# Two half-GLU chunks by seven products, and a reordered last branch, in a hybrid encoder layer on one core

## The chip, the core and the metric

The kernel runs on one core of a Trainium2 chip. The metric is device time in microseconds (us): what one execution of the whole program takes, from its start on the device to its end. Four engines matter here besides the DMA queues: PE (TensorE, matrix products), DVE (VectorE) and ACT (ScalarE), which evacuate accumulators and prepare operands, and POOL (GpSimd), which does a few elementwise operations and issues DMAs. SP only issues DMAs, here those that load weights. Each engine works through its own instructions strictly in the order in which they stand in its queue, and waits at an instruction until all that it needs is there.

## The reference

One encoder layer for 768 tokens (two request groups, of 256 and 512), model width 1024, all in float32. Of its parts only these bear on the change:

```python
y = (y_f + y_b).reshape(Bsz, L, S5_WIDTH) + s5_d * uf      # state space model
z = jax.nn.gelu(y)
s5_out = z * jax.nn.sigmoid(z @ s5_w_glu)                  # the half-GLU
# three branches (0: s5_out, 1: differential attention, 2: memory attention)
# each: merged += sigmoid(gate_n) * (branch_n @ w_branch[n])
# then x + merged @ w_out, RMSNorm, SwiGLU FFN, residual
```

`s5_w_glu` and each `w_branch[n]` are 1024 x 1024.

## The kernel before, in words

**Products.** Activations lie feature by token: a "row" is 128 features by 768 tokens, so an operand of width 1024 has eight rows, k = 0 to 7. A float32 operand is kept as a high and a low half in a rounded format, made by ACT (a copy that rounds: "hi") and DVE (the operand less that: "lo"); a product is three matmuls (`mm3`, L755 hi by hi, L756 hi by lo, L757 lo by hi), summed in PSUM.

**Weights.** `WStream` brings weights in chunks of 256 output columns. SP loads two raw tiles per chunk (128 x 1024, tag "wr", three buffers, L539). A plain chunk is split by ACT (L599) and DVE (L605), two instructions of 128 x 1024 each. A chunk of kind "w2" is split by `_split_w` for seven products: four sums and differences of weight blocks by POOL (L574, L575, L581, L583), and seven factors A11, A12, S2, S1, S3, S4, A22 by ACT (L557) and DVE (L558), 128 x 512 each, two factors to a tile, so that every second chunk's A11 lies in the tile of the last factor of the chunk before it and bears that factor's name in the trace.

**Plain chunk of the half-GLU.** For two rows m of output and two token segments (256 and 512), 8 rows k by three matmuls: 96 matmuls, 48 of 128 x 256 and 48 of 128 x 512. Chunk 0 does all four sums at once, row k by row k, since the rows of z still arrive; chunks 1 to 3 do one after the other.

**Seven products.** A chunk of 256 columns is taken as a 2 x 2 block product (output row m by the token halves h1 and h2 of 384, inner rows 0 to 3 and 4 to 7), done in seven block products instead of eight: A11 B11, A12 B21, S1 T1, S2 T2, S3 T3, S4 B22, A22 T4, where S are sums of weight blocks and T of activation blocks. That is 7 x 4 x 3 = 84 matmuls of 128 x 384. Three of the products add up in one accumulator ("brc" in `branch7`); what else must be added is added outside PSUM by DVE.

**The stages around the change**, in the order of PE: branch 2 (memory attention, `branch(2, ...)`), half-GLU (the loop after `S = rows_pair("s5o")`, four chunks), branch 0 (`branch(0, S)`), branch 1 (`branch7(1)`, four chunks by seven products), then w_out ("wo") and the FFN. z lies in DRAM (`z_scr`) and is loaded row by row and halved into `Z` (hi and lo, 0.5 z); each half-GLU row is (tanh + 1) z, put into `S` as hi and lo with a factor of 0.25 (`split_evac`, ACT L749 and DVE L750). During the half-GLU's end and branch 0, DVE and ACT prepare branch 1's T operands (`RB`) from `br_scr`, the first half of them in the buffers of Z (`ra`, `rb`) and in x1's (`rc`); `t4` holds T4's raw values.

**What sets the order.** The program is written stage by stage and a scheduler interleaves it from its own timeline; each engine then runs its queue in that fixed order. Tiles come from pools with few buffers (tag "brr" two, "glr" two, "wr" three, split weights four of each), and an instruction that takes a buffer waits until the last user of the one before has finished. `S` takes the buffers of branch 2's operand, so the first write into it waits for the end of branch 2.

## Time and profile before

| what | us |
|---|---|
| median of three runs (1741.29 to 1743.65) | 1742.41 |
| the profiled execution's own time | 1743.06 |
| span of its trace, first to last instruction | 1741.3 |
| half-GLU on PE (987.06 to 1053.90), four chunks | 66.84 |
| branch 0 on PE (1053.90 to 1120.73) | 66.83 |
| branch 1 on PE (1120.73 to 1183.75), four chunks by seven products | 63.02 |

The span is 1.8 us shorter than the time of the same execution; what lies around it is start and end. All positions below are microseconds from the start of the span. The page of the profile gives each engine's busy time; a view by windows gives the same for a stretch, with the clock that TensorE was granted (1.00 is full); a view of waits names for each engine which instruction it waited for; a timeline lists single instructions. There, "[2.12 <-DVE wl_A L558]" behind an instruction says that the engine was idle for 2.12 us before it and that an instruction of DVE at line 558 ended that wait. Names of tiles stand without their numbers ("wl_A<-wr" is a low half of an A factor made from a raw tile).

### The profile page before, as it was taken

How to read it: one execution, taken by the hardware profiler on the slowest of the kernel's cores; microseconds unless marked ns; L12 is line 12 of the kernel's file. 1: busy time of each engine (PE TensorE's matmuls, PEld its weight loads, DVE VectorE, ACT ScalarE, POOL GpSimd, SP SyncE). 2: the span in 40 equal slices, each digit the busy share in tenths (PEclk: the TensorE clock that was granted, in tenths of full speed). 3: DMA queues.
4: the chain of work that ended last, by engine and by line, in shares of the span. 5: the costliest groups of instructions: out<-in, count | busy, mean ns of one | idle time of the engine just before them, and what ended most of it. 6: DMA issues, size and time to landing. Idle time of an engine off the chain costs nothing.

```text
span 1741.3 us, 29531 instructions
## 1 busy us (share of the span) xinstructions
PE 1726.6 (99%) x11188; PEld 1608.1 (92%) x11188; DVE 1300.5 (75%) x2405; ACT 908.6 (52%) x1924; POOL 302.5 (17%) x308
## 2 busy tenths in 40 slices
PE   9999999999999999999999999999999999999999
PEld 9999988999999999999989888998889999998887
DVE  7665749699999778887886536685598777776775
ACT  7444543776767346877765434353343333334443
POOL 0000000000000100111000001341036555541130
PEclk9999999999999999999999999999999999999999
DMA  7222636755556454745653435335312323239974
GB/s 268 78 85 91 125 120 135 186 125 143 145 159 159 115 140 103 164 91 156 155 165 117 140 116 157 103 111 174 97 55 91 110 91 109 92 110 295 248 157 97
DMA packets 209213, 234.09 MB, mean 134 GB/s; under 512 B 57832, under 2 KB 173296, under 8 KB 209072
## 3 DMA queue, kind: packets, MB, share of 16 engines
q1 hardware_dynamic: 182160, 167.49, 32.0%
q0 software_dynamic: 17440, 58.34, 15.6%
q10 hardware_dynamic: 9472, 6.39, 1.3%
q8 instruction: 88, 1.44, 0.4%
q14 instruction: 53, 0.43, 0.1%
HBM read 165.78 MB, written 41.22 MB: 119 GB/s over the span
## 4 chain that ended last, share of the span: by engine, by line
PE 95%; DVE 2%; ACT 1%; issue 0%; DMA 0%; POOL 0%; SPq 0%; ACTq 0%; DVEq 0%
PE gl L755 4%; PE gl L756 4%; PE gl L757 4%; PE gate L755 3%; PE gate L756 3%; PE up L756 3%; PE gate L757 3%; PE up L755 3%; PE up L757 3%; PE dn L757 3%; PE dn L755 3%; PE dn L756 3%; PE br L755 3%; PE br L757 3%; PE br L756 3%; PE qk L755 3%
## 5 line engine op out<-in xcount | busy, mean ns | idle before, releaser
L599 ACT ACTIVATE wh<-wr 128x1024 fp32r<-128x1024 f32 x116 | 131.9, 1138 | 52.3 <-PE br L756 13.3
L605 DVE TENSOR_TENSOR wl<-wr,wh 128x1024 fp32r<-128x1024 f32 x74 | 99.2, 1342 | 63.5 <-ACT wh L599 61.7
L755 PE MATMUL gl<-H,wh 128*128 128x256 f32 (+1 forms) x384 | 132.2, 344 | 0.0
L757 PE MATMUL gl<-H,wl 128*128 128x256 f32 (+1 forms) x384 | 129.0, 336 | 0.0
L756 PE MATMUL gl<-H,wh 128*128 128x256 f32 (+1 forms) x384 | 128.7, 335 | 0.0
L603 POOL DMA_DIRECT2D wl<-wr x42 | 36.6, 872 | 483.3 <-ACT wl L602 464.1
L755 PE MATMUL qk<-wh,H 128*128 128x256 f32 x384 | 108.3, 282 | 0.0
L756 PE MATMUL qk<-wl,H 128*128 128x256 f32 x384 | 108.0, 281 | 0.0
L757 PE MATMUL qk<-wh,H 128*128 128x256 f32 x384 | 107.3, 279 | 0.0
L558 DVE TENSOR_TENSOR wl_S<-ws,wh_S 128x512 fp32r<-128x512 f32 x84 | 70.7, 863 | 26.2 <-ACT wh_S L557 26.2
L756 PE MATMUL dn<-wld,dxh 128*128 128x512 f32 x231 | 89.6, 389 | 0.0
L755 PE MATMUL dn<-whd,dxh 128*128 128x512 f32 x231 | 89.5, 389 | 0.0
L757 PE MATMUL dn<-whd,dxl 128*128 128x512 f32 x231 | 88.9, 389 | 0.0
L557 ACT ACTIVATE wh_S<-ws 128x512 fp32r<-128x512 f32 x84 | 49.5, 625 | 73.5 <-PE up L756 36.6
L757 PEld LDWEIGHTS gl<-H,wl 128*128 128x128 f32 x384 | 72.0, 188 | 8.1
L756 PEld LDWEIGHTS gl<-H,wh 128*128 128x128 f32 x384 | 72.2, 188 | 7.2
L755 PEld LDWEIGHTS gl<-H,wh 128*128 128x128 f32 x384 | 72.3, 188 | 6.9
L757 PEld LDWEIGHTS qk<-wh,H 128*128 128x128 f32 x384 | 72.6, 189 | 0.6
L755 PEld LDWEIGHTS qk<-wh,H 128*128 128x128 f32 x384 | 72.4, 188 | 0.6
L756 PEld LDWEIGHTS qk<-wl,H 128*128 128x128 f32 x384 | 72.3, 188 | 0.5
L1296 DVE TENSOR_REDUCE nm<-sc 128x1 f32<-128x512 f32 (+1 forms) x96 | 56.7, 597 | 18.1 <-PE sc L1291 17.2
L1298 ACT ACTIVATE p<-sc,nm 128x512 f32<-128x512 f32 (+1 forms) x96 | 58.8, 615 | 14.4 <-DVE nm L1296 13.9
(535 smaller groups left out, 6076.2 us busy)
## 6 DMA issues: line engine op xcount, KB each, us to landing
wr<-in_w_in_dram SPq DMA_DIRECT2D x48, 512.0 KB, 5.0
wr<-in_w_gate_up_dram SPq DMA_DIRECT2D x44, 512.0 KB, 3.6
wl<-wr POOLq DMA_DIRECT2D x42, 512.0 KB, 5.4
wr<-in_w_branch_dram SPq DMA_DIRECT2D x24, 512.0 KB, 4.5
glr<-gl_scr POOLq DMA_DIRECT2D x24, 384.0 KB, 3.5
hid_scr<-fa SPq DMA_DIRECT2D x11, 768.0 KB, 6.4
wr<-in_w_mem_kv_dram SPq DMA_DIRECT2D x16, 512.0 KB, 4.4
wr<-in_w_in_dram SPq DMA_DIRECT2D x32, 256.0 KB, 3.9
```

Of the source, the lines that this page charges most:

```text
L557: self.nc.scalar.activation(f(hi), src, AF.Copy)
L558: self.nc.vector.tensor_tensor(out=f(lo), in0=src, in1=f(hi).bitcast(F32), op=ALU.subtract)
L599: self.nc.scalar.activation(hi, r, AF.Copy)
L603: self.nc.gpsimd.dma_start(lo, r.bitcast(F32R), accum_op=ALU.add)
L605: self.sub.tensor_tensor(out=lo, in0=r, in1=hi.bitcast(F32), op=ALU.subtract)
L755: pe.matmul(ps, wh, xh, start=start, stop=False, **kw)
L756: pe.matmul(ps, wh, xl, start=False, stop=False, **kw)
L757: pe.matmul(ps, wl, xh, start=False, stop=stop, **kw)
L1296: v.tensor_reduce(out=nm[:, m : m + 1], in_=ps, axis=AX.X, op=ALU.max, negate=True)
L1298: act.activation(pm[:, 0:n], ps, AF.Exp, bias=nm[:, m : m + 1], accum_out=s1s[:, tt : tt + 1] if m == 0 else s2)
```

## The change

The line numbers in the rows below are those of the two programs; `mm3` is L755 to L757 before and L756 to L758 after, `split_evac` L749/L750 before and L750/L751 after.

1. **Half-GLU chunks 2 and 3 go by seven products** (`glu7`), with weights of kind "w2". Three products add up in "gluc", the others in tiles "p7". Evacuation is by token half: `fin(m, h)` does tanh, the gated product and hi and lo for 384 tokens.
2. **z's differences** T1 to T4 are made after each output row of chunks 0 and 1 (`z_differences(M)`, M = k = 0 to 3): POOL issues two more loads of z rows k and k + 4 into two rows of `S` that are not used yet; DVE makes T1 and T3, POOL T2 and T4 (one subtraction each, 128 x 384); ACT and DVE put them as hi and lo into `S`, into x1's buffer ("zc") and, for T4, over the part of `Z` that chunks 2 and 3 do not read.
3. **First gates in T4's tiles.** `t4` is two tiles now, which hold z's T4, then the first two gates of branch 0 (`g0`, loaded by POOL), then branch 1's T4.
4. **branch7**: accumulator tiles swapped in every odd chunk, the gated product written into the gate's tile instead of the accumulator's, the addition of row m = 0 into `merged` on POOL in chunks 0 to 2 and on DVE in chunk 3 (before: on POOL in all), S1 T1 ahead of S2 T2, and A22 T4 ahead of S4 B22 in all chunks (before: in the last alone).
5. **Factor order** for "w2" weights: A22 ahead of S4.

POOL, at the end of branch 2. Before, the last three rows of z follow the gates of branch 2 ("glr"), then come the rows that the half-GLU multiplies by ("zs"):

```order
L1517 DMA glr_1413_12412<-gl_scr23_163 128x768
L1569 DMA brr_1407_12332<-z_scr5_137 128x768
L1569 DMA brr_1408_12336<-z_scr6_138 128x768
L1569 DMA brr_1409_12340<-z_scr7_139 128x768
L1604 DMA zs_1421_12581<-z_scr0_132 128x768
```

Of the changed kernel, the same place, with the loads of `z_differences` (into "s5o", which is `S`):

```order
L1636 DMA s5o_12467<-z_scr0_132 128x768
L1637 DMA s5o_12467<-z_scr4_136 128x768
L1636 DMA s5o_12467<-z_scr1_133 128x768
L1637 DMA s5o_12467<-z_scr5_137 128x768
L1573 DMA brr_1407_12332<-z_scr5_137 128x768
L1573 DMA brr_1408_12336<-z_scr6_138 128x768
L1573 DMA brr_1409_12340<-z_scr7_139 128x768
L1651 DMA zs_1421_12590<-z_scr0_132 128x768
L574 TENSOR_TENSOR ws460_12637<-wr46_0_12355,wr46_1_12481 128x512
```

Four loads into `S` now stand ahead of rows 5, 6 and 7 of Z, and the weight sums of chunk 2 (tile numbers 46 are half-GLU chunk 2) begin right behind them.

ACT, at the same place. Before, chunk 1's weight tile (wh46 is chunk 2's) comes after the last rows of z:

```order
L599 ACTIVATE wh45_1_12474<-wr45_1_12349 128x1024
L749 ACTIVATE zhi_1400_12310<-brr_1407_12332 128x768
L749 ACTIVATE zhi_1400_12310<-brr_1408_12336 128x768
L749 ACTIVATE zhi_1400_12310<-brr_1409_12340 128x768
L599 ACTIVATE wh46_0_12596<-wr46_0_12355 128x1024
```

After:

```order
L599 ACTIVATE wh45_1_12483<-wr45_1_12349 128x1024
L557 ACTIVATE wh46_A11_12633<-wr46_0_12355 128x512
L557 ACTIVATE wh46_A11_12633<-wr46_1_12481 128x512
L750 ACTIVATE zhi_1400_12310<-brr_1407_12332 128x768
L750 ACTIVATE zhi_1400_12310<-brr_1408_12336 128x768
L750 ACTIVATE zhi_1400_12310<-brr_1409_12340 128x768
L750 ACTIVATE s5o_12467<-zd_1422_12599 128x384
```

Two factors of chunk 2 (A11 and A12, in one tile) stand ahead of rows 5 to 7 of Z, and the first difference follows them.

PE, in branch 1, where chunk 3's first product A11 B11 begins (wh54 and wh55 are chunks 2 and 3; chunk 3's A11 is the second half of the tile named after chunk 2's last factor, A22 before and S4 after). Before, right behind chunk 2's S1 T1:

```order
L756 MATMUL br_1502_13972<-rb_12988,wh54_S2_13759 128x384
L757 MATMUL br_1502_13972<-rb_12988,wl54_S2_13760 128x384
L755 MATMUL brc_1508_14055<-ra_12987,wh54_A22_13774 128x384
L756 MATMUL brc_1508_14055<-ra_12987,wh54_A22_13774 128x384
L757 MATMUL brc_1508_14055<-ra_12987,wl54_A22_13775 128x384
```

After, the two that need the high half stand at the same place, but the first that needs the low half (wl54_S4) only 38 matmuls further on, behind S2 T2 ("rc" with S2's tile), A22 T4 and S4 B22 of chunk 2:

```order
L757 MATMUL p7_1506_14067<-rb_13100,wh54_S2_13867 128x384
L758 MATMUL p7_1506_14067<-rb_13100,wl54_S2_13868 128x384
L756 MATMUL brc_1512_14163<-ra_13099,wh54_S4_13882 128x384
L757 MATMUL brc_1512_14163<-ra_13099,wh54_S4_13882 128x384
L756 MATMUL brc_1504_14039<-rc_13101,wh54_S2_13867 128x384
```

and, 34 rows further on in the same queue:

```order
L758 MATMUL p7_1506_14067<-rb_13100,wl54_S4_13883 128x384
L758 MATMUL brc_1512_14163<-ra_13099,wl54_S4_13883 128x384
L756 MATMUL brc_1512_14163<-ra_13099,wh54_S4_13882 128x384
L757 MATMUL brc_1512_14163<-ra_13099,wh54_S4_13882 128x384
L756 MATMUL brc_1504_14039<-rc_13101,wh54_S3_13875 128x384
```

So the low half of chunk 3's A11 is asked for later, while its high half is asked for at the same place.

The core of the diff:

```diff
-        self._factor(i, "S4", s4)
-        self._factor(i, "A22", A22)
+        for key, src in (("A22", A22), ("S4", s4)) if inplace else (("S4", s4), ("A22", A22)):
+            self._factor(i, key, src)
...
+            seven = nme == "w_branch1" or nme == "s5_w_glu" and c > 1
+            W.add(cols(nme, 256 * c), 8, 256, "w2" if seven else None)
...
+        zc = xp.tile([128, 8, TOK], F32R, name="zc", tag="x1")
+        q = quarters(zc)
+        ZB = {"B11": tuple(x[:, 0:4, h1] for x in Z), "B21": tuple(x[:, 4:8, h1] for x in Z),
+              "B22": tuple(x[:, 4:8, h2] for x in Z), "T2": (q[0], q[1]), "T3": (q[2], q[3]),
+              "T1": tuple(halves(x[:, 6:8]) for x in S), "T4": tuple(x[:, 0:4, h2] for x in Z)}
+        zt4 = [t4p.tile([128, 2, HT], F32, name=f"zt4{j}", tag="t4") for j in range(2)]
+
+        def z_differences(k):
+            r0, r1 = (S[j][:, 4 + k % 2].bitcast(F32) for j in range(2))
+            gp.dma_start(r0, z_scr[k])
+            gp.dma_start(r1, z_scr[k + 4])
+            (b11, b12), (b21, b22) = ((r[:, h1], r[:, h2]) for r in (r0, r1))
+            d = stg.tile([128, TOK], F32, name=uid("zd"), tag="brr")
+            t1, t3 = d[:, h1], d[:, h2]
+            v.tensor_tensor(out=t1, in0=b12, in1=b11, op=sub)
+            v.tensor_tensor(out=t3, in0=b22, in1=b12, op=sub)
+            put(ZB, "T1", k, t1, 0.5)
+            put(ZB, "T3", k, t3, 0.5)
+            gp.tensor_tensor(out=t1, in0=b22, in1=t1, op=sub)
+            gp.tensor_tensor(out=zt4[k // 2][:, k % 2], in0=b21, in1=t1, op=sub)
+            put(ZB, "T2", k, t1, 0.5)
...
+        def glu7(c):
+            w = W.get()
+            if c == 2:
+                for k in range(4):
+                    put(ZB, "T4", k, zt4[k // 2][:, k % 2], 0.5)
+            ts = [gtp.tile([128, TOK], F32, name=uid("gt"), tag="glr") for _ in range(2)]
+            zs = [z_row(2 * c + m) for m in range(2)]
+            (c11, c12), (c21, c22) = ((t[:, h1], t[:, h2]) for t in ts)
+            chain = env.psb("gluc")[:, 0:HT]
...
+            act.activation(c11, prod(w, ZB, "A11", "B11", chain), AF.Copy)
+            plus(c11, prod(w, ZB, "A12", "B21"))
+            p5 = prod(w, ZB, "S1", "T1")
+            act.activation(c22, p5, AF.Copy)
+            act.activation(c12, prod(w, ZB, "S2", "T2", chain, False), AF.Copy)
+            fin(0, h1)
+            prod(w, ZB, "S3", "T3", chain, False)
+            plus(c22, chain)
+            act.activation(c21, chain, AF.Copy)
+            fin(1, h2)
+            plus(c21, prod(w, ZB, "A22", "T4"))
+            fin(1, h1)
+            plus(c12, prod(w, ZB, "S4", "B22", p5, False))
+            fin(0, h2)
...
-        for c in range(4):
+        for c in range(2):
...
+                z_differences(M)
+        for c in range(2, 4):
+            glu7(c)
+        g0 = []
+        for m in range(2):
+            g0.append(t4p.tile([128, TOK], F32, name=uid("g0"), tag="t4"))
+            gp.dma_start(g0[m], gl_scr[m])
...
                 cs = [stg.tile([128, TOK], F32, name=uid("bs"), tag="brr") for _ in range(2)]
+                if c % 2:
+                    cs.reverse()
...
-                    v.scalar_tensor_tensor(out=cs[m], in0=gs[m], scalar=1.0, in1=cs[m], op0=add, op1=mul)
-                    (v if m else gp).tensor_tensor(out=merged[:, M], in0=merged[:, M], in1=cs[m], op=add)
+                    v.scalar_tensor_tensor(out=gs[m], in0=gs[m], scalar=1.0, in1=cs[m], op0=add, op1=mul)
+                    (v if m or c == 3 else gp).tensor_tensor(out=merged[:, M], in0=merged[:, M], in1=gs[m], op=add)
...
-                if c < 3:
-                    plus(c12, prod("S4", "B22", p5, False))
-                    merge(0)
-                    plus(c21, prod("A22", "T4"))
-                    merge(1)
-                else:
-                    plus(c21, prod("A22", "T4"))
-                    merge(1)
-                    plus(c12, prod("S4", "B22", p5, False))
-                    merge(0)
+                plus(c21, prod(w, RB, "A22", "T4"))
+                merge(1)
+                plus(c12, prod(w, RB, "S4", "B22", p5, False))
+                merge(0)
```

104 lines of the change are left out of this document (60 added, 44 removed).

## The prediction, made before the changed kernel was run

> **What bounds the kernel now.** I read the page first, for the engine that fills the span and for the chain that ends last.
>
> ```profile
> span 1741.3 us, 29531 instructions
> PE 1726.6 (99%) x11188; PEld 1608.1 (92%) x11188; DVE 1300.5 (75%) x2405; ACT 908.6 (52%) x1924; POOL 302.5 (17%) x308
> PE 95%; DVE 2%; ACT 1%; issue 0%; DMA 0%; POOL 0%; SPq 0%; ACTq 0%; DVEq 0%
> ```
>
> PE is busy 99% of the span and is 95% of the last chain, so time comes and goes with matmul work and with the few waits of PE. The view by windows shows the four half-GLU chunks, branch 0, branch 1, and two short stretches within branch 1.
>
> ```profile
> core 0: us, PE busy (x) PEld busy (x) DVE busy (x) ACT busy (x) POOL busy (x), PEclk, DMA share, GB/s
> 987.06:1003.60 16.54, 16.54 (x96) 14.50 (x95) 9.52 (x11) 7.76 (x12) 2.69 (x5) 1.00 0.72 225
> 1003.60:1020.20 16.60, 16.60 (x97) 14.69 (x96) 8.03 (x8) 6.63 (x10) 1.61 (x3) 1.00 0.32 104
> 1020.20:1036.90 16.70, 16.70 (x98) 14.78 (x97) 6.19 (x6) 5.55 (x8) 1.08 (x2) 1.00 0.37 111
> 1036.90:1053.90 17.00, 17.00 (x100) 15.01 (x99) 6.20 (x6) 6.43 (x10) 1.61 (x3) 1.00 0.43 132
> 1120.73:1183.75 63.02, 60.57 (x337) 59.72 (x336) 51.50 (x62) 33.87 (x59) 26.93 (x22) 0.97 0.38 119
> 1159.90:1163.30 3.40, 3.40 (x12) 3.40 (x12) 3.40 (x5) 1.48 (x2) 0.61 (x2) 0.50 0.49 155
> ```
>
> In the half-GLU PE never waits (busy equals the stretch, clock 1.00), and DVE has 29.9 us of work in 66.8. Branch 1 isn't full: PE waits 2.4 us there and the clock averages 0.97. The view of PE's waits, from 900 to 1260 us, and the timeline name the two waits:
>
> ```profile
> PE brc L757 <- DVE wl_A L558: 2.1, 1, 2.1
> PE brc L755 <- ACT bs L1683: 0.3, 1, 0.3
> 1156.28 0.34 PE L756 MATMUL brc<-ra,wh_A 128*128 128x384 f32 x1
> 1158.74 0.44 PE L757 MATMUL brc<-ra,wl_A 128*128 128x384 f32 x1 [2.12 <-DVE wl_A L558]
> 1155.15 3.54 DVE L558 TENSOR_TENSOR wl_A<-wr,wh_A 128x512 fp32r<-128x512 f32 x2
> 1154.24 2.22 POOL L1678 TENSOR_TENSOR merged<-merged,bs 128x768 f32<-128x768 f32 x1 [2.34 <-DVE bs L1677]
> 1156.42 1.71 POOL L574 TENSOR_TENSOR ws<-wr,wr 128x512 f32<-128x512 f32 x1
> ```
>
> Chunk 3's first product waits for its low half: DVE spent 3.54 us on two splits that lie beside two POOL operations.
>
> **Products: minus 4.3 us.** The distance between starts of equal matmuls is their price.
>
> ```profile
> 1037.21 0.28 PE L755 MATMUL glu<-zhi,wh 128*128 128x256 f32 x1
> 1040.09 0.40 PE L755 MATMUL glu<-zhi,wh 128*128 128x512 f32 x1
> 1045.55 0.28 PE L755 MATMUL glu<-zhi,wh 128*128 128x256 f32 x1
> 1150.04 0.33 PE L755 MATMUL brc<-rc,wh_S 128*128 128x384 f32 x1
> 1152.12 0.33 PE L756 MATMUL br<-ra,wh_A 128*128 128x384 f32 x1
> ```
>
> 24 matmuls of 256 columns take 2.88 us (0.120 each), 24 of 512 take 5.46 (0.2275), 12 of 384 take 2.08 (0.1733). A plain chunk is 48 x 0.120 + 48 x 0.2275 = 16.68 us, one by seven products 84 x 0.1733 = 14.56: 2.12 less, 4.24 for chunks 2 and 3 (with the windows' mean of 16.71, 4.3).
>
> **Branch 1: minus 4.3 us, of at most 4.8.** Its four chunks are 336 matmuls, 58.23 us at 0.1733, but took 63.02: 4.79 us are lost. 2.29 of them are the wait above (1156.28 to 1158.74, less one matmul). After it the clock window shows 0.50: 12 matmuls in 3.40 us, which is 1.3 us more than 2.08. A wait of 0.5 us at 1174.45 (its row says 0.3 idle, for an ACT copy) and smaller losses in the same clock phases make the rest. In the changed queue the low half of chunk 3's A11 is asked for 38 matmuls later, 6.6 us at 0.1733, against a wait of 2.3; factor A22's early place costs nothing, the tiles are the same. The wait for the ACT copy goes since the copy's accumulator is free earlier (the gated product lies in the gate's tile now) and chunk 3 has no POOL addition. What becomes late next is the same DVE queue, at chunk 3's other factors. Ends: 0 (the wait only moves) to 4.8; I take 4.3, leaving one short wait.
>
> **New work on DVE and POOL in the half-GLU: plus 0.9 us, ends 0 and 11.7.** Rows of the groups (half-GLU first, then 1092 to 1184):
>
> ```profile
> L605 DVE TENSOR_TENSOR wl<-wr,wh 128x1024 fp32r<-128x1024 f32 x8 | 9.8, 1224 | 13.0 <-ACT wh L599 13.0
> L1612 DVE SCALAR_TENSOR_TENSOR gt<-gt,zs 128x768 f32<-128x768 f32 x7 | 6.7, 956 | 18.0 <-ACT gt L1611 18.0
> L558 DVE TENSOR_TENSOR wl_A<-ws,wh_A 128x512 fp32r<-128x512 f32 x2 | 1.4, 677 | 0.0
> L1636 DVE TENSOR_TENSOR brr<-brr 128x384 f32<-128x384 f32 x1 | 0.6, 552 | 0.0
> L558 DVE TENSOR_TENSOR wl_S<-ws,wh_S 128x512 fp32r<-128x512 f32 x14 | 12.3, 894 | 10.3 <-ACT wh_S L557 10.3
> L558 DVE TENSOR_TENSOR wl_A<-wr,wh_A 128x512 fp32r<-128x512 f32 x10 | 10.9, 1110 | 4.5 <-ACT wh_A L557 4.5
> L583 POOL TENSOR_TENSOR ws<-wr,ws 128x512 f32<-128x512 f32 x4 | 5.9, 1473 | 17.5 <-DVE wl_S L558 12.1 <-DVE wl_A L558 5.4
> L1678 POOL TENSOR_TENSOR merged<-merged,bs 128x768 f32<-128x768 f32 x3 | 6.4, 2123 | 5.6 <-DVE bs L1677 5.6
> ```
>
> DVE drops four splits of 1024 (4 x 1.224 = 4.9) and eight operations of 768 (8 x 0.956 = 7.7), and takes on 14 splits of 512 (14 x 0.677 = 9.5) and 48 operations of 384 (8 differences, 12 low halves of T1, T2 and T3, 4 of T4, 8 gated products, 8 of `S`, 8 additions of products): 48 x 0.552 = 26.5. That is 23.4 more, 53.3 us in a stage of 66.84 - 4.3 = 62.5. POOL adds 16 operations to a stage where it had none: eight weight sums of about 1.48 (the row above; 11.9 us) and eight differences of 384, half of 2.123 each by their size, an estimate (8.5 us). What POOL does to DVE stands in these rows:
>
> ```profile
> 1108.52 0.68 DVE L558 TENSOR_TENSOR wl_S<-ws,wh_S 128x512 fp32r<-128x512 f32 x1
> 1109.12 0.68 DVE L1527 TENSOR_TENSOR merged<-merged,glr 128x512 f32<-128x512 f32 x1
> 1109.29 1.66 POOL L583 TENSOR_TENSOR ws<-wr,ws 128x512 f32<-128x512 f32 x1 [6.78 <-DVE wl_S L558]
> 1109.72 1.78 DVE L558 TENSOR_TENSOR wl_S<-ws,wh_S 128x512 fp32r<-128x512 f32 x1
> ```
>
> The same split took 0.68 alone and 1.78 beside a POOL operation: 1.1 us lost. On the two group rows of L558 alone the excess over 0.677 is 14 x 0.217 + 10 x 0.433 = 7.4 us, over the 19 POOL operations between 1092 and 1184 that is 0.39 for each; other DVE groups of that stretch lose too, so I take 0.55. 16 x 0.55 = 8.8, and DVE has 62.1 us to do in 62.5. That is full by busy time; but the first two rows start 0.60 apart and last 0.68 each, so operations in a queue overlap by 0.08, and about 75 operations leave 6 us to spare. PE's queue helps: T1's last product stands some 38 matmuls behind its first ones and S3 T3 last. Walking the queue, DVE's T1 row k = 3 is done about 2 us ahead of PE, T2's last row and the last rows of `S` about at the time they are asked for. T4's copies wait until PE has read Z's rows in chunk 1, and behind them on ACT and DVE stand chunk 2's evacuations; PE wants T4 only in A22 T4, so this is part of the same walk. I take one short wait, 0.9 us.
>
> The Trainium skill, page "SBUF — State Buffer", section "SBUF: two separate sides", speaks against the change: a DVE operation with two SBUF inputs and a POOL operation exclude each other for the whole instruction, the later one blocks fully. The trace agrees: the 1.78 us row ends 0.55 us after the POOL operation beside it. Taken literally for all 16 it would cost DVE up to POOL's 20.4 us, not 8.8, and PE some 11 us; the mean excess of the group rows speaks for less, since PSUM-bound operations and gaps in DVE's queue take a part.
>
> **Loads ahead of Z's last rows: plus 0.6 us, ends 0 and 3.7.**
>
> ```profile
> 987.64 0.54 POOL L1569 DMA_DIRECT2D brr<-z_scr  x1 [18.17 <-DVE zlo L750]
> 991.08 0.85 ACT L749 ACTIVATE zhi<-brr 128x768 fp32r<-128x768 f32 x1 [0.84 <-DMA brr<-z_scr]
> 994.11 0.85 ACT L749 ACTIVATE zhi<-brr 128x768 fp32r<-128x768 f32 x1 [0.30 <-DMA brr<-z_scr]
> ```
>
> Row 5 of Z is issued at 987.64 and used by ACT from 991.08. Now four loads into `S` stand ahead of it; they wait for PE's end of branch 2 (987.06), and behind them wait rows 5 to 7 and the "zs" rows. They are 4 x 0.39 MB, 7 us at the 225 GB/s of the first window's row, so row 5 reaches ACT near 998.3 and its low half DVE near 1000. PE asks for row 5 after five rows of 2.09 us and the 12 early matmuls of chunk 2, 987.06 + 10.4 + 2.1 = 999.6. ACT's two factors ahead of it aren't later than this (the copy at 995.43 in the old queue waited for a PE release; two of 0.62 fit). So 0 to 2.4 us of wait, with a half clock behind it 1.3 more; I take 0.6.
>
> **Nothing for the rest.** ACT gains about as many operations as DVE, but works 26.4 of 66.8 us there by the windows, so 23 more still leave room. The first gates' loads are moved, not added. SP's loads keep size and order. The end of branch 1 has one POOL addition less in its last chain.
>
> **Sum.** 1743.06 - 4.3 - 4.3 + 0.9 + 0.6 = 1736.0 on the profiled execution (the 1.8 us around its span don't change), which is 0.65 above the median of the runs: 1735.3, I say 1735.5.
>
> **Half clock.** The wait of 2.3 us was followed by 3.4 us at 0.50. The Trainium skill, page "TensorE: Matmul & The Clock Gate", section "What's actually happening", gives an idle window of about 3.4 us as what throttles; by it a 2.3 us wait would stay free and branch 1's term would be 2.8 instead of 4.3, with 1737.0 as the time. The row of 1159.90 differs, and the measurement decides.
>
> **Rivals.** *(a) No new wait at all*: -4.3 - 4.8 = 1733.3 to 1734. For it: the spare 6 us. *(b) Row loads decide*: a wait of 2.4 with its half clock, 3.7 instead of 0.6, gives 1738.6. For it: the 7 us of loads ahead; against: PE asks 2 us later. *(c) Branch 1's wait moves to another factor*: 0 instead of -4.3, 1739.8. For it: DVE there has 51.5 of 63.0 us as before; against: 38 matmuls of room. *(d) Slower: DVE becomes the bound of the half-GLU.* Each of the 16 POOL operations costs 1.1 us, as at 1109.72: 17.6 instead of 8.8, DVE 70.9 us in 62.5. PE then waits 8.4, and two of the waits bring a half clock of 1.3 to 1.7: 11.7 in all in place of 0.9, 1736 + 10.8, as a median 1746.2. It decides from about 0.6 per operation on, if the overlap isn't there, else from 0.95. That is what the SBUF page's rule gives too. *(e) That the change doesn't do what it says* I exclude: the queue has 24 matmuls fewer.
>
> **How the numbers follow.** Forecast 0.47, (a) 0.17, (b) 0.13, (c) 0.12, (d) 0.11. Less than 0.2% (3.5 us) from 1742.4 can't be told from no change: under 1738.9 is faster. The forecast, (a) and half of (b), which lies at that bound, are faster: 0.70. The other half of (b), (c) and the low edge of (d) are within: 0.20. Slower, above 1745.9, is the rest of (d): 0.10. The range goes from (a) with 0.3 of scatter, 1733.0, to 1742.5: past (b) and (c), and into (d), whose upper part is left out.
>
> **What would show it.** Half-GLU to branch 0's first matmul 62.5 to 64 us, with PE's waits on zhi, s5o, zc or zlo summing to 0 to 2.5; branch 1 58.3 to 59.5 us with PEclk 1.00 and no wait on wl_A; DVE 55 to 63 us busy in the half-GLU; POOL's splits' neighbours on DVE at 1.0 us in the mean. The prediction is wrong if PE waits more than 3 us in the half-GLU, if the wait on wl_A stays, or if the stages around these two change.

## The result, and the profile after

The changed kernel is slower: 1754.52 us median of five runs (1752.92 to 1755.14) against 1742.41, a ratio of 1.0068 with a 95% interval of 1.0057 to 1.0080. That lies outside the forecast range and on the other side of no change. The profiled execution took 1752.92 us, 9.9 more than the 1743.06 of before, where the forecast had 7.1 less. First the page, the lines that answer to those of before:

```profile
span 1751.2 us, 29624 instructions
PE 1725.0 (99%) x11164; PEld 1607.5 (92%) x11164; DVE 1332.2 (76%) x2456; ACT 923.8 (53%) x1962; POOL 326.4 (19%) x331
PE 92%; DVE 3%; DMA 1%; issue 1%; ACT 1%; POOL 0%; SPq 0%; ACTq 0%; DVEq 0%; POOLq 0%
```

PE has 24 matmuls fewer and is 1.6 us less busy, although some of its time is half clock; the span grew all the same, and of the last chain PE has 92% now where it had 95%. So PE waits. The view by windows of the changed kernel (columns as before: the stretch and its length, busy time of PE, PEld, DVE, ACT and POOL with counts, granted clock, DMA share, GB/s) takes the half-GLU in four pieces, then branch 0 up to branch 1's first matmul, branch 1, and the start of w_out:

```profile
986.52:1020.00 33.48, 33.48 (x196) 29.83 (x195) 25.96 (x32) 16.32 (x30) 17.82 (x22) 1.00 0.65 218
1020.00:1039.50 19.50, 15.59 (x80) 13.65 (x79) 18.89 (x25) 11.65 (x24) 13.10 (x11) 1.00 0.30 88
1039.50:1042.90 3.40, 3.35 (x10) 3.35 (x11) 1.06 (x2) 0.29 (x1) 1.89 (x3) 0.50 0.67 226
1042.90:1053.93 11.03, 9.35 (x54) 9.03 (x53) 8.59 (x16) 8.45 (x16) 1.09 (x2) 1.00 0.69 215
1053.93:1125.04 71.11, 70.39 (x410) 62.28 (x409) 54.23 (x93) 31.15 (x53) 14.25 (x20) 1.00 0.45 143
1125.04:1190.93 65.89, 58.98 (x337) 58.02 (x335) 53.99 (x64) 35.90 (x60) 29.28 (x28) 0.99 0.40 126
1190.93:1196.30 5.37, 5.37 (x13) 4.21 (x14) 4.39 (x6) 0.84 (x1) 0.00 (x0) 0.50 1.01 385
```

Between 1020 and 1039.5 us DVE is busy 18.89 of 19.50 us while PE loses 3.9. The half clock comes twice: at 1039.5, and right after branch 1, where thirteen matmuls take 5.37 us. Stage by stage, from PE's first matmul of each:

| stage | before | after | difference | forecast |
|---|---|---|---|---|
| start of the half-GLU | 987.06 | 986.52 | -0.5 | 0 |
| half-GLU and branch 0 | 133.67 | 138.52 | +4.9 | -2.8 |
| branch 1 | 63.02 | 65.89 | +2.9 | -4.3 |
| w_out to the end of the span | 557.55 | 560.27 | +2.7 | 0 |
| span | 1741.3 | 1751.2 | +9.9 | -7.1 |

The view of PE's waits from 900 to 1270 us (total, times, longest; "p" are the tiles "p7") has these lines for these stages, where before there were 2.1 and 0.3:

```profile
PE wo L756 <- ACT bs L1771: 4.5, 1, 4.5
PE p L756 <- DVE bs L1614: 1.8, 1, 1.8
PE p L756 <- DVE gt L1614: 1.7, 1, 1.7
PE p L757 <- DVE zlo L751: 1.6, 2, 1.0
PE gluc L756 <- ACT zc L750: 1.3, 1, 1.3
PE p L756 <- ACT zhi L750: 0.8, 1, 0.8
PE br L756 <- DVE g L1528: 0.7, 1, 0.7
PE brc L756 <- ACT bs L1768: 0.6, 1, 0.6
PE gluc L757 <- DVE zc L751: 0.2, 1, 0.2
```

The old wait on wl_A is gone, as forecast. In its place there are six in the half-GLU (gt, zlo twice, zc twice, zhi; 5.6 us in all), one at branch 0's start, and three in branch 1 and behind it, of which w_out's is the longest.

**In the half-GLU** the timeline shows a chain from POOL over ACT to PE, for the last difference T2 (k = 3):

```profile
1033.50 2.73 POOL L1645 TENSOR_TENSOR zd<-s5o,zd 128x384 f32<-128x384 f32 x1 [0.77 <-DVE s5o L751]
1036.26 0.52 ACT L750 ACTIVATE zc<-zd 128x384 fp32r<-128x384 f32 x1 [3.09 <-POOL zd L1645]
1036.84 0.44 PE L756 MATMUL gluc<-zc,wh_S 128*128 128x384 f32 x1 [1.31 <-ACT zc L750]
```

A subtraction of 384 elements, for which I had reckoned 1.1 us, took POOL 2.73, beside DVE operations that left only 0.27 us idle. T4's last row follows it over the same engines: the waits on zhi and zlo, 2.4 us in all, are for T4's rows.

**In branch 1** the wait of 1.8 us is the old exclusion of DVE and POOL at another place; DVE first, then POOL, then PE:

```profile
1174.64 2.09 DVE L558 TENSOR_TENSOR wl_A<-wr,wh_A 128x512 fp32r<-128x512 f32 x1
1174.34 1.85 POOL L1761 TENSOR_TENSOR merged<-merged,glr 128x768 f32<-128x768 f32 x1 [2.92 <-DVE glr L1760]
1177.86 0.45 PE L756 MATMUL p<-mgd,wh_A 128*128 128x384 f32 x1 [1.83 <-DVE bs L1614]
```

PE's next accumulator is freed by an addition (L1614) that stands behind that split in DVE's queue.

**At the end of branch 1** w_out's first matmul waits for an ACT copy (c21, L1771) that empties an accumulator. The timeline of ACT, with two rows of DVE and PE's among it:

```profile
1185.71 0.85 ACT L1750 ACTIVATE glr<-glr 128x768 f32<-128x768 f32 x1 [1.76 <-DMA glr<-gl_scr]
1186.46 1.98 ACT L599 ACTIVATE wh<-wr 128x1024 fp32r<-128x1024 f32 x2
1187.53 1.23 DVE L605 TENSOR_TENSOR wl<-wr,wh 128x1024 fp32r<-128x1024 f32 x1 [1.24 <-ACT wh L599]
1188.67 0.95 DVE L1761 TENSOR_TENSOR merged<-merged,glr 128x768 f32<-128x768 f32 x1
1189.66 0.84 ACT L1736 ACTIVATE mgd<-merged 128x768 fp32r<-128x768 f32 x1 [1.22 <-DVE merged L1761]
1190.41 0.47 ACT L1771 ACTIVATE bs<-brc 128x384 f32<-128x384 f32 x1
1190.93 0.79 PE L756 MATMUL wo<-wh,mgd 128*128 128x512 f32 x1 [4.46 <-ACT bs L1771]
```

The copy needs only the product S3 T3, whose last matmul began at 1186.14, but in ACT's queue it stands behind the copy of merged row 6, which needs DVE's addition into that row. That addition stands in DVE's queue behind a split of w_out's weights (L605), which waits for ACT's half of it, and ACT does that only after the tanh of the next gate, which waits for its load. PE had S3 T3 last; before the change S4 B22 was last, and the copy had been done by then.

### The profile page after: what moved, and what is told of

Same layout as the page of the kernel before. It is cut to its first block, busy times and chain, and to the rows that moved or that the text cites. A ratio compares the mean times of both kernels' runs of the same rounds, so it can differ in the third digit from the quotient of the medians.

```text
span 1751.2 us, 29624 instructions
## 1 busy us (share of the span) xinstructions
PE 1725.0 (99%) x11164; PEld 1607.5 (92%) x11164; DVE 1332.2 (76%) x2456; ACT 923.8 (53%) x1962; POOL 326.4 (19%) x331
## 4 chain that ended last, share of the span: by engine, by line
PE 92%; DVE 3%; DMA 1%; issue 1%; ACT 1%; POOL 0%; SPq 0%; ACTq 0%; DVEq 0%; POOLq 0%
PE gl L756 4%; PE gl L758 4%; PE gl L757 4%; PE gate L756 3%; PE gate L758 3%; PE up L758 3%; PE gate L757 3%; PE up L757 3%; PE up L756 3%; PE dn L758 3%; PE dn L756 3%; PE dn L757 3%; PE qk L756 3%; PE qk L757 3%; PE qk L758 3%; PE br L756 2%
## 5 line engine op out<-in xcount | busy, mean ns | idle before, releaser
L599 ACT ACTIVATE wh<-wr 128x1024 fp32r<-128x1024 f32 x112 | 127.6, 1141 | 41.9 <-PE br L757 13.5
L756 PE MATMUL gl<-H,wh 128*128 128x256 f32 (+1 forms) x384 | 132.2, 344 | 0.0
L605 DVE TENSOR_TENSOR wl<-wr,wh 128x1024 fp32r<-128x1024 f32 x70 | 93.9, 1342 | 48.8 <-ACT wh L599 47.1
L758 PE MATMUL gl<-H,wl 128*128 128x256 f32 (+1 forms) x384 | 129.0, 336 | 0.0
L757 PE MATMUL gl<-H,wh 128*128 128x256 f32 (+1 forms) x384 | 128.7, 335 | 0.0
L756 PE MATMUL qk<-wh,H 128*128 128x256 f32 x384 | 107.9, 281 | 0.0
L757 PE MATMUL qk<-wl,H 128*128 128x256 f32 x384 | 107.7, 280 | 0.0
L758 PE MATMUL qk<-wh,H 128*128 128x256 f32 x384 | 107.0, 279 | 0.0
L757 PE MATMUL dn<-wld,dxh 128*128 128x512 f32 x231 | 89.6, 389 | 0.0
L756 PE MATMUL dn<-whd,dxh 128*128 128x512 f32 x231 | 89.5, 389 | 0.0
L758 PE MATMUL dn<-whd,dxl 128*128 128x512 f32 x231 | 88.9, 389 | 0.0
L758 PEld LDWEIGHTS gl<-H,wl 128*128 128x128 f32 x384 | 72.0, 188 | 8.1
L757 PEld LDWEIGHTS gl<-H,wh 128*128 128x128 f32 x384 | 72.2, 188 | 7.2
L756 PEld LDWEIGHTS gl<-H,wh 128*128 128x128 f32 x384 | 72.3, 188 | 6.8
L758 PEld LDWEIGHTS qk<-wh,H 128*128 128x128 f32 x384 | 72.3, 188 | 0.6
L756 PEld LDWEIGHTS qk<-wh,H 128*128 128x128 f32 x384 | 72.3, 188 | 0.6
L757 PEld LDWEIGHTS qk<-wl,H 128*128 128x128 f32 x384 | 72.3, 188 | 0.5
```

The source lines that it names most:

```text
L599: self.nc.scalar.activation(hi, r, AF.Copy)
L605: self.sub.tensor_tensor(out=lo, in0=r, in1=hi.bitcast(F32), op=ALU.subtract)
L756: pe.matmul(ps, wh, xh, start=start, stop=False, **kw)
L757: pe.matmul(ps, wh, xl, start=False, stop=False, **kw)
L758: pe.matmul(ps, wl, xh, start=False, stop=stop, **kw)
```

## The experiments

Times are medians, the ratio is to the kernel before on the same chip, with its 95% interval. All kernels are built anew by the scheduler, so an edit can also move rows that it doesn't name.

| kernel | us | before | ratio |
|---|---|---|---|
| b7_only | 1746.41 | 1741.70 | 1.0026 (1.0017 to 1.0035) |
| glu7_only | 1747.52 | 1741.70 | 1.0031 (1.0021 to 1.0041) |
| cs_merge | 1756.66 | 1741.70 | 1.0086 (1.0071 to 1.0101) |
| no_differences | 1744.36 | 1741.70 | 1.0013 (1.0004 to 1.0022) |
| zdiff_dve | 1752.19 | 1741.39 | 1.0060 (1.0045 to 1.0075) |
| no_pool_diff | 1750.77 | 1741.39 | 1.0054 (1.0039 to 1.0069) |
| b7_pool_last | 1744.52 | 1741.39 | 1.0017 (1.0008 to 1.0027) |
| b7_no_gs_fac | 1741.17 | 1741.39 | 1.0002 (0.9992 to 1.0011) |
| b7_dve_add | 1740.07 | 1742.19 | 0.9993 (0.9984 to 1.0003) |
| best_a | 1745.13 | 1742.19 | 1.0018 (1.0009 to 1.0027) |
| best_b | 1753.42 | 1742.19 | 1.0066 (1.0052 to 1.0079) |
| best_c | 1757.51 | 1742.19 | 1.0089 (1.0076 to 1.0103) |
| best_d | 1742.66 | 1741.58 | 1.0005 (0.9996 to 1.0014) |
| after_no_g0 | 1752.63 | 1741.58 | 1.0066 (1.0053 to 1.0080) |
| best_f | 1743.40 | 1741.83 | 1.0004 (0.9995 to 1.0012) |
| best_g | 1743.48 | 1741.83 | 1.0008 (0.9999 to 1.0017) |

### The two halves of the change, each alone

**b7_only** takes the half-GLU back to four plain chunks (no `glu7`, no `z_differences`, no `g0`) and keeps the last branch and the factor order:

```diff
-            seven = nme == "w_branch1" or nme == "s5_w_glu" and c > 1
+            seven = nme == "w_branch1"
...
-        branch(0, S, gates=g0)
+        branch(0, S)
```

> The changed last branch and the changed factor order alone, the half-GLU as before (four plain chunks, no differences, no gates in T4's tiles). Theory A (two separate losses: the half-GLU by DVE's queue, the last branch by its own new order and by gate tiles that are held longer): the last branch loses here too what it lost in the changed kernel, 2.9 us to w_out's first matmul and about 2.7 us of half clock behind it, so about 1748 us. Rival B (the last branch's waits are a sequel of the half-GLU): the old losses of 4.8 us are gone and no new ones come, about 1738 us.

**glu7_only** keeps the half-GLU's part and takes `branch7` and the factor order back.

```diff
-        for key, src in (("A22", A22), ("S4", s4)) if inplace else (("S4", s4), ("A22", A22)):
+        for key, src in (("S4", s4), ("A22", A22)):
...
-                if c % 2:
-                    cs.reverse()
...
-                    v.scalar_tensor_tensor(out=gs[m], in0=gs[m], scalar=1.0, in1=cs[m], op0=add, op1=mul)
+                    v.scalar_tensor_tensor(out=cs[m], in0=gs[m], scalar=1.0, in1=cs[m], op0=add, op1=mul)
```

> The seven-product chunks of the half-GLU, z's differences and the gates in T4's tiles, with the last branch and the factor order as before. Theory A: only the half-GLU's loss, 1742.4 + 4.3 = 1746.7 us, with PE waiting about 7 us between 1020 and 1055 us and the old wait of 2.1 us in the last branch back. Rival B: the sequel is in the last branch whatever its code, 1751 to 1754 us.

Both lose, 0.26% and 0.31%, and the sum, 0.57%, is the lower end of the whole change's interval. So there are two losses, and each part is slower by itself; theory A holds and B falls. In b7_only the wait at w_out is 2.9 us instead of 4.5. The timeline of its end:

```profile
1183.01 0.84 ACT L1676 ACTIVATE mgd<-merged 128x768 fp32r<-128x768 f32 x1 [0.69 <-DVE merged L1701]
1183.76 0.47 ACT L1711 ACTIVATE bs<-brc 128x384 f32<-128x384 f32 x1
1184.29 0.50 PE L756 MATMUL wo<-wh,mgd 128*128 128x512 f32 x1 [2.88 <-ACT bs L1711]
```

```profile
1172.10:1175.50 3.40, 3.40 (x13) 3.40 (x12) 3.40 (x5) 2.02 (x3) 0.54 (x1) 0.53 0.77 271
```

It is the same queue. The second fence, a window of the same kernel, tells why the wait is shorter: here the 1.8 us wait within the branch brought 3.4 us of half clock at once, so PE reached the end 1.6 us later and waited 1.6 less. From the end of that wait to w_out's first matmul both kernels take 13.1 us: the end is set by ACT's and DVE's queue, not by PE. The branch takes 65.5 us here, against 63.0 before the change.

### What of the last branch it is

**cs_merge** undoes one thing of the changed kernel, the tile into which the gated product goes:

```diff
-                    v.scalar_tensor_tensor(out=gs[m], in0=gs[m], scalar=1.0, in1=cs[m], op0=add, op1=mul)
-                    (v if m or c == 3 else gp).tensor_tensor(out=merged[:, M], in0=merged[:, M], in1=gs[m], op=add)
+                    v.scalar_tensor_tensor(out=cs[m], in0=gs[m], scalar=1.0, in1=cs[m], op0=add, op1=mul)
+                    (v if m or c == 3 else gp).tensor_tensor(out=merged[:, M], in0=merged[:, M], in1=cs[m], op=add)
```

> The changed kernel with one thing undone: the last branch's gated product goes into the accumulator's tile again, not into the gate's. Theory A1 (the gate's tile is held until the addition into merged, so the next gates load late, their tanh blocks ACT's queue and with it the copy that w_out's first matmul waits for): the gates of chunk 3 load about 3.4 us earlier, the wait of 4.5 us falls to about 1, the half clock behind it goes, 1748 to 1749 us. Rival A2 (S3 T3 as the last product makes that wait, through the long chain behind it): the wait stays above 3.5 us, 1753 to 1755 us.

The wait at w_out fell from 4.5 to 2.9 us, but waits of 2.0 (a split of DVE at chunk 3's first product, as before the change), 2.6 and 0.7 stood in the branch, and the kernel was slower still. A1 falls: here the last two gates' tanh instructions wait for no load (3.36 and 1.76 us in the changed kernel), and the copy is late all the same. A2's time, 1753 to 1755, is missed too, on the other side.

**b7_pool_last** and **b7_no_gs_fac** are b7_only with one and two things undone:

```diff
b7_pool_last
-                    (v if m or c == 3 else gp).tensor_tensor(out=merged[:, M], in0=merged[:, M], in1=gs[m], op=add)
+                    (v if m else gp).tensor_tensor(out=merged[:, M], in0=merged[:, M], in1=gs[m], op=add)
b7_no_gs_fac
-        for key, src in (("A22", A22), ("S4", s4)) if inplace else (("S4", s4), ("A22", A22)):
+        for key, src in (("S4", s4), ("A22", A22)):
...
-                    v.scalar_tensor_tensor(out=gs[m], in0=gs[m], scalar=1.0, in1=cs[m], op0=add, op1=mul)
+                    v.scalar_tensor_tensor(out=cs[m], in0=gs[m], scalar=1.0, in1=cs[m], op0=add, op1=mul)
```

> The changed last branch with the half-GLU as before, and one thing of the branch undone: in its chunk 3 the addition of row m = 0 into merged is on POOL again, not on DVE. By that the ACT copy that w_out's first matmul waits for stands ahead of the copies of merged in ACT's queue instead of between them; S3 T3 stays the last product. Theory E1 (the wait of 2.9 us is that copy's place behind a copy of merged): the wait falls under 1 us, 1743 to 1744 us against 1746.4. Rival E2 (the wait belongs to S3 T3 as last product): it stays at 2.5 to 3 us, 1746 us.

> The changed last branch with the half-GLU as before, and without two of its parts: the gated product goes into the accumulator's tile, and the factor S4 stands ahead of A22 again. The queue then has S3 T3 ahead of S4 B22 in chunk 3, as before the change. Theory E2 (S3 T3 as last product makes the wait at w_out): no wait there and no half clock behind it, 1742 to 1744 us. Rival E3 (the wait is made by the swapped accumulators or by A22 T4 ahead of S4 B22): it stays, 1746 us. If the old wait of 2.1 us at chunk 3's first product is back, the factor order or the gate tile is what had removed it.

b7_pool_last lies between its theories: the wait fell from 2.88 to 1.84 us, since the copy, now ahead of the copies of merged, still waits for DVE's addition. b7_no_gs_fac has, in the view of waits from 980 to 1200 us:

```profile
PE brc L758 <- DVE wl_A L558: 1.7, 1, 1.7
PE brc L756 <- ACT bs L1704: 1.6, 1, 1.6
```

No wait at w_out, no half clock, and the time of before. So the branch's loss goes with the order in which S3 T3 comes last, in which its evacuation meets the others at the end (E2); E1's place in ACT's queue is some 1.0 us of the wait. The other runs agree: all eight kernels whose PE queue has S3 T3 last, the changed one among them, wait 1.8 to 4.7 us at w_out, and none of the nine that have S4 B22 last shows that wait. The queues show that either of the two edits alone, on the old branch, puts S3 T3 last; which of them weighs how much was not run. What the change had removed, the wait on wl_A, is back at once.

**b7_dve_add** puts all additions into merged on DVE (`v` in place of `(v if m or c == 3 else gp)`).

> The last branch of b7_no_gs_fac with all additions into merged on DVE, none on POOL (the half-GLU as before the change). Theory F1 (the wait at chunk 3's first product, 1.8 us there, is the splits of DVE that POOL's additions lengthen by 1.1 us each): three POOL additions fewer, three DVE additions of 0.95 more, the wait falls under 0.7 us, 1739 to 1740.5 us, faster than before by 1 to 2. Rival F2 (DVE has no room for the additions, 51 of 63 us): other waits of the same size, 1741 to 1743 us.

The wait didn't fall, it was 2.0 us, against F1; one of 1.6 us went instead. The time is at the lower edge of no difference.

### What of the half-GLU it is

**no_differences** leaves out z's differences and takes z's own blocks in place of T1 to T4 (so chunks 2 and 3 have other values); products, weight sums and evacuations stay.

```diff
+        ZB.update({"T1": ZB["B12"], "T2": ZB["B11"], "T3": ZB["B21"], "T4": ZB["B22"]})
...
-                z_differences(M)
```

> The changed kernel with z's blocks B12, B11, B21 and B22 in place of T1 to T4, so that the differences, their loads and their 16 copies are left out and the values of chunks 2 and 3 of the half-GLU are others; products, weight sums and evacuations stay. Theory A (DVE's queue, filled by the differences and slowed by POOL, makes the half-GLU's waits): its PE waits of 7 us fall under 1.5 us, 8 us less in all, about 1746 us. Rival C (the seven products' own evacuations and weight sums are what PE waits for): PE still waits 4 us or more there, above 1750 us.

Its window over the old half-GLU, and, from the view of waits, the only one of PE from 980 to 1125 us:

```profile
987.06:1053.90 66.84, 66.84 (x390) 62.51 (x389) 45.02 (x55) 36.11 (x61) 20.50 (x23) 1.00 0.47 156
```

```profile
PE br L756 <- DVE g L1528: 1.4, 1, 1.4
```

PE is busy the whole stretch at full clock. The six waits hang on the differences, as theory A says, and the seven products, their sums and evacuations cost no wait there. That it is DVE's queue, filled and slowed by POOL, isn't shown by this run, which takes work from ACT, POOL and the DMA queues too. Even so this kernel is 0.13% slower than before: the last branch's waits, 1.8 us in it and 3.0 at w_out, are all there.

**zdiff_dve** and **no_pool_diff** ask whether it is DVE's work or POOL beside it. In the first, all subtractions are DVE's; in the second POOL's are left out (T2 from T1's values, T4 from a loaded block, so that chunks 2 and 3 have other values).

```diff
zdiff_dve
-            gp.tensor_tensor(out=t1, in0=b22, in1=t1, op=sub)
-            gp.tensor_tensor(out=zt4[k // 2][:, k % 2], in0=b21, in1=t1, op=sub)
+            v.tensor_tensor(out=t1, in0=b22, in1=t1, op=sub)
+            v.tensor_tensor(out=zt4[k // 2][:, k % 2], in0=b21, in1=t1, op=sub)
no_pool_diff
+            gp.dma_start(zt4[k // 2][:, k % 2], z_scr[k + 4][:, h1])
```

> The changed kernel with all four of z's subtractions on DVE, none on POOL. In the changed kernel POOL operations lengthened DVE operations of the half-GLU by 11.0 us, 0.69 for each of its 16. Theory D1 (DVE's time decides, POOL's exclusion included): eight POOL operations fewer give DVE 5.5 us back, eight subtractions more take 3.8, so PE's waits in the half-GLU fall from 7 to about 5 us, 1752 to 1753 us. Rival D2 (POOL's relief of DVE is worth its price): DVE has 3.8 us more and PE waits 10 us or more, 1757 us or above.

> The changed kernel with POOL's eight subtractions left out (T2 is then put from T1's values, T4 from a loaded block of z), so that DVE and ACT have the same instructions as in the changed kernel and the values of chunks 2 and 3 are others. Theory D1: DVE gets 5.5 us back, PE's waits in the half-GLU fall from 7 to about 2 us, 1748 to 1749 us. Rival D3 (DVE's own instruction count decides, POOL beside it costs nothing): waits as before, 1754 us.

Moved to DVE, the subtractions cost no more than on POOL (1.0060 against 1.0068, the intervals overlap): POOL is no relief, D2 falls. Left out, the time over the kernel before went from 12.1 to 9.4 us, by half of what was expected, and the intervals overlap here too (1.0054 against 1.0068). D1's 1748 to 1749 us lie at the interval's lower edge or below it, so its size is missed. D3 doesn't fall: its 1754 us lie within the interval, and PE's waits up to branch 0's start are 6.0 us (2.6 on one of DVE's additions, 2.4 at branch 0's start) where the changed kernel has 6.3. So neither run shows that POOL's subtractions decide.

**best_a** is the change with zdiff_dve's edit, without the two edits of b7_no_gs_fac, and with all additions on DVE.

> All of the change except what the runs showed to cost time: z's subtractions on DVE, the additions into merged on DVE, the gated product in the accumulator's tile, the factor S4 ahead of A22. Theory (the half-GLU's loss and the last branch's loss add): zdiff_dve's 1752.2 less the 6.6 us between the whole kernel's last branch and one that waits for nothing at w_out, 1745 to 1747 us. Rival (the half-GLU's delay of DVE goes on into the last branch): 1749 us or more.

The two losses add, as the theory says: 1745.13, 2.9 us above the kernel before where the changed kernel was 12.1. Of the half-GLU one long wait is left, and the timeline gives it a cause that none of the theories had (ACT, then DVE, then PE):

```profile
1038.25 0.85 ACT L1522 ACTIVATE g<-g 128x768 f32<-128x768 f32 x1 [2.85 <-DMA g<-gl_scr]
1039.00 0.62 ACT L557 ACTIVATE wh_S<-ws 128x512 fp32r<-128x512 f32 x1
1039.65 0.69 DVE L558 TENSOR_TENSOR wl_S<-ws,wh_S 128x512 fp32r<-128x512 f32 x1 [2.64 <-ACT wh_S L557]
1044.60 0.69 PE L756 MATMUL p<-zhi,wh_S 128*128 128x384 f32 x1 [4.10 <-DVE gt L1614]
```

ACT stands at the tanh of a gate of branch 0, a stage ahead of its time, whose load had to wait for T4's tile; chunk 3's weight factors stand behind it.

**best_d** and **after_no_g0** leave the gates out of T4's tiles, in best_a and in the changed kernel:

```diff
-            g0.append(t4p.tile([128, TOK], F32, name=uid("g0"), tag="t4"))
-            gp.dma_start(g0[m], gl_scr[m])
...
-        branch(0, S, gates=g0)
+        branch(0, S)
```

> best_a without the first gates in T4's tiles: branch 0 loads all its gates into the gates' own two tiles again. In best_a ACT's tanh of the second of these gates waited 2.85 us for its load (which waits for T4's copies), the split of chunk 3's weights stood behind it on ACT and DVE, and PE waited 4.1 us with 6.8 us of half clock behind. Theory G1 (that tanh at the head of ACT's queue makes the wait): the wait goes, no half clock before 1060 us, 1737.5 to 1739.5 us, faster than before. Rival G2 (DVE is late by itself, or the gates of branch 0 now come late): PE waits 3 us or more between 1036 and 1070 us, 1743 to 1746 us.

> The changed kernel without the first gates in T4's tiles, everything else as changed. Theory G1: in the changed kernel the same tanh waited 3.98 us for its load at 1043.77 us; without it the wait of 1.7 us at 1049.66 goes, the waits of 1027 to 1040 us, before it, stay (they are DVE's and POOL's), 1751 to 1753 us. Rival G3 (the gates' place decides the whole loss of the half-GLU): 1747 us or less. Rival G2: 1754 us or more.

In best_d the wait of 4.1 us fell to 1.9 and the time over the kernel before from 2.9 to 1.1 us, which is no measurable difference to that kernel (the intervals of best_a and best_d overlap). So the tanh made about half of that wait. The other half is G2's: 1.9 us, with half clock behind it, and 1.8 at branch 0's start (1.4 in best_a) stay, more than the 3 us that G2 had named, and G1's time is missed. In the changed kernel, where DVE is later than that tanh, it is worth about 1 us (12.1 to 11.1 over the kernel before), within the intervals.

**best_f** and **best_g** put the weight sums on DVE too, of the half-GLU and then of branch 1 as well:

```diff
-        gt = self.nc.gpsimd.tensor_tensor
+        gt = (self.nc.vector if i in (46, 47) else self.nc.gpsimd).tensor_tensor
```

> best_d with the eight weight sums of half-GLU chunks 2 and 3 on DVE, so that POOL does no elementwise operation in the half-GLU at all. In best_d they lengthened DVE operations there by 8.6 us, and one sum took POOL 5.6 us beside a busy DVE, with ACT's factor waiting 4.85 us for it. Theory D1 (POOL beside DVE gives nothing: each operation takes DVE about what DVE itself needs for it): DVE gains 8.6 and takes on 8 x 0.6 = 4.8, the chain over POOL is gone, the waits of 2.0 at 1042 and 1.9 at 1065 us fall by 2 us and more in all, 1738 to 1740.5 us. Rival D2 (POOL's sums were a relief): DVE later, 1743.5 us or more.

> best_f with branch 1's sixteen weight sums on DVE too. Theory D1: the wait of 2.2 us at its chunk 3's first product, where a split of DVE stands beside a sum of POOL, goes, 1736 to 1739 us. Rival D2: DVE (about 51 us busy of 63 there, and 9.6 more) is late at other factors, 1740 us or more.

Neither moves the time. PE's waits of best_f from 980 to 1125 us:

```profile
PE p L756 <- DVE gt L1614: 1.8, 1, 1.8
PE br L756 <- DVE glr L1528: 1.4, 1, 1.4
PE p L756 <- ACT gt L1673: 0.5, 1, 0.5
PE gluc L756 <- ACT gt L1674: 0.4, 1, 0.4
```

They are 4.1 us, which is what the 24 matmuls fewer had given (4.24); in best_d they were 3.7. D1's time is missed in both: without any elementwise operation of POOL there, PE waits as long. D2's 1743.5 us is not told apart from the 1743.40 measured. best_g got rid of the wait at branch 1's chunk 3, as D1 said, and has one of 3.0 us on an ACT copy there.

**best_b** and **best_c** take the low halves of the weight factors (best_c: of two more weight chunks) off DVE by an accumulating DMA.

```diff
+        if i in (46, 47):
+            self.nc.scalar.activation(f(lo), src, AF.Copy, scale=-1.0)
+            self.nc.gpsimd.dma_start(f(lo), src.bitcast(F32R), accum_op=ALU.add)
```

> best_a with the 14 low halves of the half-GLU's weight factors made without DVE (ACT writes the negative high half, an accumulating DMA of POOL's queue adds the raw value). DVE loses 14 x 0.6 = 8.4 us of work in the half-GLU. Theory (DVE's time between 1003 and 1043 us makes the half-GLU's waits): its PE waits fall under 2 us, 1739 to 1741 us, faster than before. Rival (latency: the longer way of the factors, a DMA each, comes late to PE, or ACT becomes the bound): PE waits on ACT or on DMAs in the half-GLU, 1745 us or more.

> best_b with the low halves of the weights of half-GLU chunk 1 and of branch 0's first chunk made by accumulating DMAs too: four DVE operations of 1.22 us fewer. Theory as for best_b: 1 to 2 us below best_b, above all by the waits from 1047 us on and in branch 0. Rival (the waits that are left are not DVE's): as best_b, within 1 us.

Both are misses, by latency; best_b's longest wait in the half-GLU:

```profile
PE p L762 <- DMA wl_A<-wr: 3.3, 1, 3.3
```

No version is measurably faster than the kernel before; b7_dve_add, which has none of the half-GLU's part, comes nearest.

## Why the prediction was wrong

**Products, -4.3 us: right.** Where nothing disturbs them (no_differences) half-GLU and branch 0 take 131.0 us, 1.4 of them a wait, against 133.67: 4.1 us less of work, with 24 matmuls fewer.

**Branch 1, -4.3 us: failed at "What becomes late next is the same DVE queue, at chunk 3's other factors".** The wait on wl_A went as forecast. But the step looked only at the place of the old wait and took the end for granted ("The end of branch 1 has one POOL addition less in its last chain"). The changed queue has S3 T3 last, with its copy on ACT behind merged's; that costs 4.5 us of wait and the half clock behind it. "The wait for the ACT copy goes since the copy's accumulator is free earlier (the gated product lies in the gate's tile now)" left out the other side: the gate's tile is held longer, and the last two gates' tanh instructions wait 3.36 and 1.76 us for their loads (2.17 and 0.75 before). By cs_merge this isn't what decides. Of the last branch's 5.6 us of loss (2.9 in it, 2.7 behind it) none was in the sum.

**New work in the half-GLU, +0.9 us: mis-sized, and by a step of its own.** With branch 0 the stage lost 9.1 us (138.52 against 133.67 less 4.24) where the forecast allowed 1.5 for the work and the loads. The price of POOL's operations was near: 0.55 us of DVE each as forecast, 0.69 as measured (11.0 us in all, each DVE operation from 987 to 1054 us less what its form takes beside an idle POOL). What failed is "DVE has 62.1 us to do in 62.5", with operations whose overlap is to "leave 6 us to spare", as a sum over the stage. DVE was busy 54.5 us of the 67.4 up to branch 0's first matmul, less than forecast, and PE waited 5.6 us all the same, where the prediction had called itself wrong from 3 on. DVE has 25.96 us of work in the first 33.5 us, and in the next 19.5 us it has 18.89, since the differences of k = 2 and 3, T4's copies and both chunks' factors fall due together; the spare time lies where nothing is ready. In the walk through the queue T1 was in time, as forecast, since no wait on s5o came. But "T2's last row and the last rows of `S` about at the time they are asked for" took POOL's subtraction as 1.1 us; it took 2.73 and stood between two engines. And T4's copies, "part of the same walk", made 2.4 us of the waits.

**Gates in T4's tiles: "moved, not added", costed at nothing.** Wrong: the tanh of a gate, early in ACT's queue and late in its load, is worth about 2 us of wait in best_a; in the changed kernel, where DVE was late anyway, about 1, which the intervals don't separate from nothing.

**Loads ahead of Z's last rows, +0.6 us: not needed.** The waits have no row there; the first 33.48 us of the half-GLU are busy throughout, and row 5's copy ran at 995.93, ahead of the 998.3 reckoned.

**The rivals.** (d) named DVE, behind which PE has four of the six waits (3.5 of 5.6 us), and its rule, POOL excludes DVE, holds: POOL's operations lengthened DVE's by 11.0 us in the changed kernel, and in best_f, where POOL has none from 987 to 1054 us, no DVE operation is longer than its form takes. The Trainium skill, page "SBUF — State Buffer", section "SBUF: two separate sides", says that the loser blocks for the whole instruction. The rows show such a block for POOL (2.73 us at 1033.50) as well as for DVE (2.09 at 1174.64). But (d) too summed over the stage, at 1.1 us for each where 0.69 were measured, and its 1746.2 us are 8.3 short of the result. best_f shows that the rule isn't the deciding point: without POOL's operations the time is the same (1.0004 against 1.0005), with DVE doing that work itself. That the end of branch 1 would wait was no rival at all. The chance of 0.10 for slower was too small, since much of the new work was put on the two engines that the trace showed excluding each other.

**Half clock.** It came twice on top of the waits, at 1039.5 and at 1190.93 us. (d) had reckoned with two, both in the half-GLU.

**What stays open.** Which of the two edits of the last branch weighs how much. And why best_f's waits of 4.1 us remain with POOL out of the way: they follow DVE's additions (L1614) and ACT's copies, which were not taken apart further. That the differences make the half-GLU's waits is shown by leaving them out; that it is DVE's work falling due at once, rather than the order of the queues or the few buffers that the differences pass through, is read from the windows, and no run changed it alone.

## What to carry to other kernels

An engine's spare time counts only where its work is ready and due: sum busy time over the stretch between a release and the need, not over the stage, and put helpers that exclude each other (here POOL and DVE) down as one engine. When an edit removes a wait, read the end of the changed queue as closely as the place of the wait: which product is now last, and what stands ahead of its evacuation in a queue that runs in order. An operation that the scheduler puts early into a queue (a gate's tanh) holds up its engine until its load lands, and everything behind it waits along.

## What the runs showed of the hardware that was not expected

DVE can hold POOL up for longer than one instruction. In best_d two weight sums of one shape, for which the kernel before took 1.30 to 2.51 us each (four of them), took 7.1 together, and one of them 5.61 beside DVE operations that followed each other without a gap. It ended 1.23 us after the only one of them that reads PSUM had begun (L1614 at 1027.89), near the 1.30 us of the shortest of those four; this is one case. The group, and the instruction:

```profile
L574 POOL TENSOR_TENSOR ws<-wr,wr 128x512 f32<-128x512 f32 x2 | 7.1, 3542 | 5.1 <-DVE wl_S L558 4.0 <-DVE zlo L751 1.1
```

```profile
1023.51 5.61 POOL L574 TENSOR_TENSOR ws<-wr,wr 128x512 f32<-128x512 f32 x1 [4.00 <-DVE wl_S L558]
```

Whether a wait of PE brings the half clock is not told by its length. The same wait of 2.00 us, at chunk 3's first product, was followed by half clock in best_f and by none in b7_dve_add. Of each the instruction and a window behind the wait (the granted clock is the third number from the end), best_f first:

```profile
1159.92 0.45 PE L758 MATMUL brc<-ra,wl_A 128*128 128x384 f32 x1 [2.00 <-DVE wl_A L558]
```

```profile
1160.50:1163.90 3.40, 3.40 (x13) 3.38 (x12) 3.40 (x5) 1.95 (x3) 0.91 (x2) 0.50 0.63 225
```

```profile
1157.28 0.44 PE L758 MATMUL brc<-ra,wl_A 128*128 128x384 f32 x1 [2.00 <-DVE wl_A L558]
```

```profile
1157.28:1166.00 8.72, 8.72 (x50) 8.72 (x51) 8.72 (x11) 5.97 (x10) 5.03 (x3) 1.00 0.43 152
```

The fourteenth matmul behind the waiting one began 4.12 us after it in best_f and 2.54 in b7_dve_add. So a wait of 2 us costs 2 or 3.6 us, depending on something that its length doesn't show.
